# Gathered rows on the memory of the output weights, seven gate-and-up buffers and three transpose banks in a mixture-of-experts stage

## Chip, cores and metric

The kernel runs on one NeuronCore of a Trainium2 chip. The metric is the device time of one execution in microseconds (us). The engines are TensorE (PE; its weight loads are PEld), VectorE (DVE), ScalarE (ACT), GpSimd (POOL) and SyncE (SP), which issues most DMAs.

## What is computed

One step of a hybrid decoder layer for 1024 prompt tokens and 32 sample tokens (1056 in all, width 1024, fp32): an input projection, two parallel attentions, an output projection with a residual, and a two-level mixture of experts. Only the last part bears on the change:

```python
def hier_moe(x, w_rg, b_rg, w_re, b_re, w_g, w_u, w_d):
    ...                                    # a group of 8 experts per token, then its top 2 experts
    dense_gate = jnp.sum(jax.nn.one_hot(ids, N_EXPERTS) * gates[..., None], axis=1)
    hg = jnp.einsum('nd,edf->nef', x, w_g)          # 32 experts, d = 1024, f = 256
    hu = jnp.einsum('nd,edf->nef', x, w_u)
    act = jax.nn.silu(hg) * hu * dense_gate[..., None]
    return jnp.einsum('nef,efd->nd', act, w_d)
...
h = x + mixed @ w_out
return h + hier_moe(rms_norm(h, g_ffn), ...)
```

## The kernel before

Everything runs once, unrolled. A planner of the tile framework orders the instructions of each engine while the program is built: what comes earlier in the program goes first, unless its model of the engines says that it isn't ready and something later is. At run time each engine and each DMA queue goes through its list in order.

**Projection and routing.** The loop over `order` (sample tile first, then eight prompt tiles of 128 rows) runs `project(t)`: the attention's output times `w_out` in three matmuls per chunk (L1328 to L1330, weights `woh`, `wol`), plus the residual, into `h`, which is stored to a DRAM table `hnd` and to the output `yd`. The last tile's stores go through POOL (L1341). L1344 is a small power on POOL for the norm of each tile. `route(t)` (L1346 on) finds two experts per token and their places in lists of 96 slots per expert. `woh` and `wol` fill 64 KB of each partition; when the last projection has been traced, `p3w` closes, and pool `xw2` opens on the upper half of that memory, with two buffers for gate and up weights and two for down weights.

**Weights.** `weights(e, part)` (L1253) loads one expert: part 0 is gate and up (two DMAs of 1 MB into one 16 KB buffer, L1274), part 1 is down (1 MB, L1267). There are six buffers of each, four in `xw` and two in `xw2`, used in turn, so that load n waits for the last use of expert n-6. `HOLD` lets the first load of each part that is issued in the loop wait for the slot table `its`: a one-column copy on POOL into the buffer (L1266, L1272), behind which SP's queue stands.

**Group 0.** The first 32 slots of four experts are known two tiles early. `early_slots` gathers their rows, and after the last tile PE does `turn_rows`, `first_products`, `gated`, `turn_hidden`, `second_products` for them (L1478 and L1486 in the rows below that stand at 1073 to 1078 us). The result `yo0` lies in a buffer of tag `xt` in pool `fp` and is added to the output rows by a scattering DMA on POOL with an adding write (`add_rows`, L1489).

**Groups 1 to 23.** Pool `ep` opens where `fp` and `sm` lay when `p3` closes. Its first tiles are the six `xg` buffers, so `xg` 1 and 2 lie on the two `xt` buffers, one of which holds `yo0`. For each group of 128 slots:

- `fetch` (L1449, POOL) gathers 128 rows of `hnd` into `xg`. Slots without a token gather nothing, so each of the six buffers is zeroed once, on DVE (L1599), before its first gather.
- `turn_rows`: two times four transposes on PE into a bank of PSUM (tag `tr`, two banks; L1458), each followed by a copy with a factor on DVE into a half of `xT` (L1459).
- `turned_hidden` of the group before: two transposes on PE into a `tr` bank (L1478), one copy on DVE to `aTe` (L1479).
- `first_products`: 64 matmuls (L1466) into `acc` (two banks); `gated`: one ACT (L1470) and one DVE instruction (L1472), which read `acc`.
- `down` of the group before: 32 matmuls (L1486) into `S` (two times two banks), ACT writes `yo` (L1620, four buffers), POOL adds it to the output (L1489). Adds go one after the other, since they write the same tensor.

A group uses one or two experts: four groups use three. `units_of` asks for the weights when a group first needs them; the planner puts them on SP's queue.

Of the kernel before, what the change touches and what calls it, by code (L numbers as in the profile page):

```python
# [6 lines left out]
F32 = mybir.dt.float32  # L7
# [8 lines left out]
P = 128  # L16
# [106 lines left out]
def build(tc, a, upto=99, dbg=None):  # L123
# [1120 lines left out]
    xw = p4.enter_context(tc.tile_pool(name="xw", bufs=1, reuse_waits="tile"))  # L1244
    WG, WD = (4, 6), (4, 6)
    xw2 = []
    NEARLY = ((1, 4), (1, 5), (0, 4))
    HOLD = (1, 1)
    XG, YO = 6, 4
    SPREAD = (1, 1, 2, 3, 4, 4, 6, 6)  # L1250
    loaded = [0, 0]

    def weights(e, part, hold=None):  # L1253
# [3 lines left out]
        lim = (WG, WD)[part]  # L1257
        first = n % lim[1] < lim[0]
        pool, bufs = (xw, lim[0]) if first else (xw2[0], lim[1] - lim[0])

# [47 lines left out]
    def project(t):  # L1308
# [34 lines left out]
        V.tensor_scalar(s1[:n, 1:2], s1[:n, 0:1], 1.0 / D, EPS, op0=ALU.mult, op1=ALU.add)  # L1343
        G.tensor_tensor(out=s1[:n, 2:3], in0=s1[:n, 1:2], in1=nhalf[:n, 0:1], op=ALU.pow)  # L1344

# [177 lines left out]
    for i, t in enumerate(order):  # L1523

        pj = project(t)
        last, route_ = route_, None
        step(pj)
        if last:
            step(last)
        step(pj)  # L1530
        if last:
            step(last)
        step(pj)
        route_ = route(t, *hs[t])
        step(route_)
        step(pj)
        if last:
            step(last)
        if i == len(order) + EARLY:
            early_slots()  # L1540
        if i == NT:

            p3w.close()
            xw2.append(p4.enter_context(tc.tile_pool(name="xw2", bufs=1, side="right", reuse_waits="tile")))
            for part, e in NEARLY:
                W_[(part, e)] = weights(8 * (e % 4) + e // 4, part)
        for part, e in ahead.get(i, ()):
            W_[(part, e)] = weights(8 * e, part)

    step(route_)  # L1550
    x0T = turn_rows(xg0s[0], lambda: fp.tile([P, KC, P], F32, name="mx"))
# [28 lines left out]
    V.tensor_scalar(cnti[:, 1:2], cnti[:, 0:1], 7, None, op0=ALU.arith_shift_right)  # L1580
    hid = fp.tile([P, D], F32, name="xt")
    gated(it0[:, 0], gu0, hid[:, :256], hid[:, 256:512])
# [3 lines left out]
    second_products(py0, aT0, u0)  # L1586
    yo0 = fp.tile([P, D], F32, name="xt")
    for q in range(2):
# [3 lines left out]

    psum(2)
    ep = p4.enter_context(tc.tile_pool(name="ep", bufs=2, reuse_waits="tile"))

    def fetch(it, new=False):
        xg = ep.tile([P, D], F32, name="xg", bufs=XG)
        if new:
            V.memset(xg, 0.0)  # L1599
        fetch_to(it, xg)  # L1600
        return it, xg

    def new_xT():
# [12 lines left out]
    def down(it, aT, units):  # L1616
        py = big()
        second_products([py[:, :512], py[:, 512:]], aT, units)
        yo = ep.tile([P, D], F32, name="yo", bufs=YO)
        S.activation(yo, py, AF.Copy, scale=it[:, 1:2].bitcast(F32))  # L1620
        add_rows(it, yo)
# [17 lines left out]

    fetched = {g: fetch(its[:, g], True) for g in (1, 2)}  # L1640
    add_rows(it0[:, 0], yo0)
    behind = None
# [17 lines left out]
    with tc.If(npass > 0):  # L1660
        nrow = 32 * OVF
        ini = ep.tile([P, D], F32, name="xg", bufs=XG)[:, :3 * (nrow // P)].bitcast(I32).rearrange("p (i c) -> p i c", c=3)
        G.iota(ini[:, :, 0], pattern=[[1, nrow // P]], base=0, channel_multiplier=nrow // P)
        V.tensor_scalar(ini[:, :, 0], ini[:, :, 0], 127, None, op0=ALU.bitwise_and)
        inif = ep.tile([P, D], F32, name="xg", bufs=XG)[:, :nrow // P]
        V.tensor_scalar(inif, ini[:, :, 0], float(NTOK), None, op0=ALU.add)
# [58 lines left out]
```

## Time and profile before

| | us |
|---|---|
| median of 3 runs (1405.79 to 1407.11) | 1406.47 |
| profiled execution | 1398.5 |
| its span, first to last instruction | 1396.7 |
| PE busy in the span (90%) | 1258.1 |
| DVE busy (57%) | 801.4 |
| POOL busy (32%) | 447.7 |

The profile is of one execution. Starts are counted from the span's start. A line of a timeline has the start, the duration (of a merged run of equal instructions, to its end), the engine, the line of the kernel, the operation, what it writes and reads, how many, and in brackets how long the engine stood idle before it and what released it. A letter q behind an engine's name is its instruction queue.

### The profile page before, as it was taken

What the parts mean: (1) busy time and instruction counts of PE and PEld (TensorE: products, weight loads), DVE (VectorE), ACT (ScalarE), POOL (GpSimd) and SP (SyncE); (2) the same over time, 40 slices, a digit from 0 to 9 for tenths busy, and PEclk for the clock granted to TensorE, in tenths of its full rate; (3) what the DMA queues carried; (4) which work ended last, traced back from release to release, by engine and by line L of the source; (5) the groups of instructions that cost most, each with busy time, mean ns of one, the idle gap of its engine ahead of it and who ended that gap; (6) DMA issues with size and microseconds to landing.
All of it is one profiled execution on the core that took longest, in us unless ns stands there. A gap on an engine that the chain in (4) does not pass through costs nothing. (4 is left out here: it accounts for less than half of the span.)

```text
span 1396.7 us, 24892 instructions
## 1 busy us (share of the span) xinstructions
PE 1258.1 (90%) x9393; PEld 842.8 (60%) x9393; DVE 801.4 (57%) x2232; ACT 561.7 (40%) x1240; POOL 447.7 (32%) x505
## 2 busy tenths in 40 slices
PE   7999999997789689898889989999998799999994
PEld 5877675875467576675675776768884233333331
DVE  5545996969987677676655556836653311122210
ACT  5533666895432365544445555722221011111110
POOL 1012233254336534335237644322121212222101
PEclk9999999998899799999999999999999899999997
DMA  7223004133325865666558653357636699999962
GB/s 245 68 90 123 25 24 121 48 110 74 99 98 142 233 245 214 232 212 234 178 199 283 222 167 129 92 188 289 248 117 229 235 386 396 396 389 384 391 216 36
DMA packets 114294, 272.60 MB, mean 195 GB/s; under 512 B 52600, under 2 KB 52856, under 8 KB 101880
## 3 DMA queue, kind: packets, MB, share of 16 engines
q1 hardware_dynamic: 81248, 180.84, 35.5%
q0 software_dynamic: 26272, 87.58, 20.0%
q10 hardware_dynamic: 6648, 2.54, 0.7%
q8 instruction: 75, 1.23, 0.3%
q14 instruction: 51, 0.42, 0.1%
HBM read 234.33 MB, written 44.44 MB: 200 GB/s over the span
## 5 line engine op out<-in xcount | busy, mean ns | idle before, releaser
L532 PE MATMUL acc<-wh,xh 128*128 128x512 f32 x432 | 174.6, 404 | 13.8 <-ACT wh L508 13.8
L533 PE MATMUL acc<-wh,xl 128*128 128x512 f32 x432 | 172.0, 398 | 0.0
L1466 PE MATMUL acc<-wg,xT 128*32 128x512 f32 x1472 | 164.3, 598 | 0.0
L941 ACT ACTIVATE mk<-mk,mx 128x256 f32<-128x256 f32 (+7 forms) x128 | 99.0, 774 | 83.2 <-DVE mx L939 78.8
L535 PE MATMUL acc<-wl,xh 128*128 128x512 f32 x320 | 126.5, 395 | 0.0
L1472 DVE SCALAR_TENSOR_TENSOR ac<-acc,its,sg 128x256 f32<-128x256 f32 x23 | 15.8, 688 | 165.1 <-ACT sg L1470 165.1
L532 PEld LDWEIGHTS acc<-wh,xh 128*128 128x128 f32 x432 | 82.5, 191 | 46.3 <-ACT wh L508 22.1
L1466 PEld LDWEIGHTS acc<-wg,xT 128*32 128x32 f32 x1472 | 45.6, 110 | 101.8 <-issue 101.5
L533 PEld LDWEIGHTS acc<-wh,xl 128*128 128x128 f32 x432 | 82.5, 191 | 17.3 <-issue 1.2
L1470 ACT ACTIVATE sg<-acc,its 128x256 f32<-128x256 f32 x23 | 10.9, 473 | 194.7 <-PE acc L1466 194.7
L1486 PE MATMUL S<-wd,aTe 128*32 128x512 f32 x736 | 83.2, 592 | 0.6 <-DVE aTe L1479 0.6
L1105 PE MATMUL tr<-cst,pg 128*128 128x128 f32 x512 | 78.9, 287 | 0.5 <-DVE ql L407 0.4
L937 PE MATMUL tr<-KS,qh 128*128 128x512 f32 (+3 forms) x192 | 74.0, 390 | 1.5 <-DVE aT L865 0.7
L959 POOL TENSOR_SCALAR mk<-mk,rl 128x128 f32<-128x128 f32 (+7 forms) x64 | 49.1, 780 | 69.2 <-DVE rl L951 64.1
L1449 POOL DMA_INDIRECT xg<-s_hn,its x23 | 23.5, 1022 | 140.3 <-PE tr L1458 122.8
L877 PE MATMUL tr<-cst,mk 128*128 128x128 f32 x432 | 64.9, 281 | 3.9 <-POOL mk L959 2.4
L535 PEld LDWEIGHTS acc<-wl,xh 128*128 128x128 f32 x320 | 60.7, 190 | 11.7
L1489 POOL DMA_INDIRECT out_o_y_dram<-yo,its x23 | 36.2, 1576 | 91.7 <-ACT yo L1620 52.1
L1105 PEld LDWEIGHTS tr<-cst,pg 128*128 128x128 f32 x512 | 61.6, 147 | 6.4 <-issue 1.2
L938 PE MATMUL tr<-KS,ql 128*128 128x512 f32 (+3 forms) x192 | 65.1, 353 | 0.0
L1459 DVE TENSOR_TENSOR xT<-tr,gc 128x512 f32<-128x512 f32 x46 | 29.7, 686 | 60.6 <-PE tr L1458 60.6
L877 PEld LDWEIGHTS tr<-cst,mk 128*128 128x128 f32 x432 | 48.5, 142 | 21.8 <-issue 13.5
(447 smaller groups left out, 2913.9 us busy)
## 6 DMA issues: line engine op xcount, KB each, us to landing
wg<-in_w_exp_gate_dram SPq DMA_DIRECT2D x32, 1024.0 KB
wg<-in_w_exp_up_dram SPq DMA_DIRECT2D x32, 1024.0 KB
wd<-in_w_exp_down_dram SPq DMA_DIRECT2D x32, 1024.0 KB
wr<-in_w_in_dram SPq DMA_DIRECT2D x56, 256.0 KB
xt<-in_x_prompt_dram SPq DMA_DIRECT2D x16, 512.0 KB
s_mix<-mo SPq DMA_DIRECT2D x16, 256.0 KB
qn<-s_qa SPq DMA_DIRECT2D x8, 512.0 KB
raw<-in_w_out_dram SPq DMA_DIRECT2D x16, 256.0 KB
```

The lines of the kernel that those rows point to most:

```text
L532: T_.matmul(ps, lhsT=xh[t][:, kc, :], rhs=wh[kc], start=kc == 0 and t < NT - 1, stop=False)
L533: T_.matmul(ps, lhsT=xl[t][:, kc, :], rhs=wh[kc], start=False, stop=t == NT - 1 and kc == KC - 1)
L535: T_.matmul(ps, lhsT=xh[t][:, kc, :], rhs=wl[kc], start=False, stop=kc == KC - 1)
L877: T_.transpose(pt[:, (j - b) * P:(j - b + 1) * P], src[:, j * P:(j + 1) * P], ident)
L937: T_.matmul(sp[:, :c1 - c0], lhsT=T.qh[:, h * P:(h + 1) * P], rhs=KS[:, h, c0:c1], start=True, stop=False)
L938: T_.matmul(sp[:, :c1 - c0], lhsT=T.ql[:, h * P:(h + 1) * P], rhs=KS[:, h, c0:c1], start=False, stop=True)
L941: S.activation(mk[:, :W], mk[:, :W], AF.Exp, bias=mx[:, h:h + 1], scale=-1.0, accum_out=T.ll[:, h:h + 1])
L959: G.tensor_scalar(ex[s][:, :W], ex[s][:, :W], T.rl[:, 2 * u + s:2 * u + s + 1], 1.0, op0=ALU.mult, op1=ALU.mult)
L1105: T_.transpose(pt[:, c * P:(c + 1) * P], raws[bb][:, o_:o_ + P], ident)
L1466: T_.matmul(gu[c:c + m, :].rearrange("p (u f) -> p u f", u=2), lhsT=xT[:, k, c:c + m], rhs=wg[:, :, k, :], start=k == 0, stop=k == KC - 1)
L1486: T_.matmul(py[q][c:c + m], lhsT=aT[:, k, c:c + m], rhs=wd[:, k, q * 512:(q + 1) * 512], start=k == 0, stop=k == 1)
L1489: G.indirect_dma_start(out=yd, out_offset=bass.IndirectOffsetOnAxis(ap=it[:, 0:1], axis=0), in_=yo, in_offset=None, compute_op=ALU.add, bo ...
```

## The change

Gathered rows get a pool of their own, `xg`, on the lower quarter of the memory that `woh` and `wol` held (four buffers of 4 KB; six before, in `ep`). The first two are zeroed on POOL by instructions that the planner must put behind the last L1344 on that engine; buffers 3 and 4 are zeroed on POOL too, where the planner likes. `yo` has two buffers in place of four, and the first of them is allocated before all else in `ep`. `hid` and `yo0` of group 0 use the tag `mh` in place of `xt`. Gate and up weights get a seventh buffer, in `ep`, behind `yo`, that is, over `hT`, both `mh` buffers and one `mx` buffer of `fp`. Loads 5 and 6 of gate and up are asked for between the first two gathers and `add_rows(it0)`, load 5 with the wait for `its`, and the count of held loads is lowered. `psum(3, 1)` gives three banks to `tr` and one to `acc`.

```diff
@@ -1242,11 +1242,11 @@
     p4 = ExitStack()
     cq = p4.enter_context(tc.tile_pool(name="cq", bufs=1))
     xw = p4.enter_context(tc.tile_pool(name="xw", bufs=1, reuse_waits="tile"))
-    WG, WD = (4, 6), (4, 6)
+    WG, WD = (4, 6, 7), (4, 6, 6)
     xw2 = []
     NEARLY = ((1, 4), (1, 5), (0, 4))
     HOLD = (1, 1)
-    XG, YO = 6, 4
+    XG, YO = 4, 2
     SPREAD = (1, 1, 2, 3, 4, 4, 6, 6)
     loaded = [0, 0]
 
@@ -1255,8 +1255,8 @@
         n = loaded[part]
         loaded[part] += 1
         lim = (WG, WD)[part]
-        first = n % lim[1] < lim[0]
-        pool, bufs = (xw, lim[0]) if first else (xw2[0], lim[1] - lim[0])
+        i = n % lim[2]
+        pool, bufs = (xw, lim[0]) if i < lim[0] else (xw2[0], lim[1] - lim[0]) if i < lim[1] else (xw2[2], lim[2] - lim[1])
 
         def src(nm):
             return a[nm][0, e] if isinstance(e, int) else a[nm][0, bass.ds(e, 1)].rearrange("o k n -> (o k) n")
@@ -1341,7 +1341,9 @@
             st.dma_start(dst[r0:r0 + n], h[:n])
         V.tensor_tensor(out=s1[:n, 0:1], in0=s1[:n, 0:1], in1=s1[:n, 1:2], op=ALU.add)
         V.tensor_scalar(s1[:n, 1:2], s1[:n, 0:1], 1.0 / D, EPS, op0=ALU.mult, op1=ALU.add)
-        G.tensor_tensor(out=s1[:n, 2:3], in0=s1[:n, 1:2], in1=nhalf[:n, 0:1], op=ALU.pow)
+        last_pow[0] = G.tensor_tensor(out=s1[:n, 2:3], in0=s1[:n, 1:2], in1=nhalf[:n, 0:1], op=ALU.pow).ins
+
+    last_pow = [None]
 
     def route(t, h, s1):
 
@@ -1542,11 +1544,17 @@
 
             p3w.close()
             xw2.append(p4.enter_context(tc.tile_pool(name="xw2", bufs=1, side="right", reuse_waits="tile")))
+            xw2.append(p4.enter_context(tc.tile_pool(name="xg", bufs=XG, side="right", reuse_waits="tile")))
             for part, e in NEARLY:
                 W_[(part, e)] = weights(8 * (e % 4) + e // 4, part)
         for part, e in ahead.get(i, ()):
             W_[(part, e)] = weights(8 * e, part)
 
+    with tc.issue_after(last_pow[0]):
+        xgs = []
+        for _ in range(2):
+            xgs.append(xw2[1].tile([P, D], F32, name="xg"))
+            G.memset(xgs[-1], 0.0)
     step(route_)
     x0T = turn_rows(xg0s[0], lambda: fp.tile([P, KC, P], F32, name="mx"))
     step(route_)
@@ -1578,27 +1586,34 @@
     cnti = cq.tile([P, 2], I32, name="cnti")
     V.tensor_scalar(cnti[:, 0:1], cnt[:, 32:33], float(P - 1 - CAP), None, op0=ALU.add)
     V.tensor_scalar(cnti[:, 1:2], cnti[:, 0:1], 7, None, op0=ALU.arith_shift_right)
-    hid = fp.tile([P, D], F32, name="xt")
+    hid = fp.tile([P, D], F32, name="mh")
     gated(it0[:, 0], gu0, hid[:, :256], hid[:, 256:512])
     aT0 = hid[:, 512:768].rearrange("p (k n) -> p k n", k=2)
     turn_hidden(hid[:, 256:512], aT0)
     py0 = [acc(), acc()]
     second_products(py0, aT0, u0)
-    yo0 = fp.tile([P, D], F32, name="xt")
+    yo0 = fp.tile([P, D], F32, name="mh")
     for q in range(2):
         S.activation(yo0[:, q * 512:(q + 1) * 512], py0[q], AF.Copy, scale=it0[:, 0, 1:2].bitcast(F32))
     p3.close()
 
 
-    psum(2)
+    psum(3, 1)
     ep = p4.enter_context(tc.tile_pool(name="ep", bufs=2, reuse_waits="tile"))
 
     def fetch(it, new=False):
-        xg = ep.tile([P, D], F32, name="xg", bufs=XG)
-        if new:
-            V.memset(xg, 0.0)
+        if xgs:
+            xg = xgs.pop(0)
+        else:
+            xg = xw2[1].tile([P, D], F32, name="xg")
+            if new:
+                G.memset(xg, 0.0)
         fetch_to(it, xg)
         return it, xg
+
+
+    yos = [ep.tile([P, D], F32, name="yo", bufs=YO)]
+    xw2.append(ep)
 
     def new_xT():
         return ep.tile([P, KC, P], F32, name="xT")
@@ -1616,7 +1631,7 @@
     def down(it, aT, units):
         py = big()
         second_products([py[:, :512], py[:, 512:]], aT, units)
-        yo = ep.tile([P, D], F32, name="yo", bufs=YO)
+        yo = yos.pop() if yos else ep.tile([P, D], F32, name="yo", bufs=YO)
         S.activation(yo, py, AF.Copy, scale=it[:, 1:2].bitcast(F32))
         add_rows(it, yo)
 
@@ -1638,6 +1653,8 @@
         return units
 
     fetched = {g: fetch(its[:, g], True) for g in (1, 2)}
+    W_[(0, 5)], W_[(0, 6)] = (weights(8 * (n % 4) + n // 4, 0, its[:, 1, 0:1] if n == 5 else None) for n in (5, 6))
+    held[0] -= 1
     add_rows(it0[:, 0], yo0)
     behind = None
     for g in range(1, NG + 2):
@@ -1659,10 +1676,10 @@
     npass = nc.values_load(cnti[0:1, 1:2], min_val=0, max_val=8)
     with tc.If(npass > 0):
         nrow = 32 * OVF
-        ini = ep.tile([P, D], F32, name="xg", bufs=XG)[:, :3 * (nrow // P)].bitcast(I32).rearrange("p (i c) -> p i c", c=3)
+        ini = xw2[1].tile([P, D], F32, name="xg")[:, :3 * (nrow // P)].bitcast(I32).rearrange("p (i c) -> p i c", c=3)
         G.iota(ini[:, :, 0], pattern=[[1, nrow // P]], base=0, channel_multiplier=nrow // P)
         V.tensor_scalar(ini[:, :, 0], ini[:, :, 0], 127, None, op0=ALU.bitwise_and)
-        inif = ep.tile([P, D], F32, name="xg", bufs=XG)[:, :nrow // P]
+        inif = xw2[1].tile([P, D], F32, name="xg")[:, :nrow // P]
         V.tensor_scalar(inif, ini[:, :, 0], float(NTOK), None, op0=ALU.add)
         V.tensor_copy(ini[:, :, 0], inif)
         V.memset(ini[:, :, 1:], 0)
```

## Rows read from the trace of the kernel before

**Rows 1.** Windows, all engines: stretch; busy us (instructions) per engine; clock; DMA share; GB/s

```profile
1075.00:1110.00 35.00, 20.68 (x166) 7.26 (x162) 9.00 (x12) 1.85 (x3) 9.71 (x9) 0.80 0.63 206
...
1180.00:1215.00 35.00, 33.98 (x306) 12.04 (x302) 6.70 (x12) 4.76 (x6) 6.69 (x6) 1.00 1.02 391
...
1343.00:1346.00 3.00, 3.00 (x36) 0.91 (x32) 0.57 (x1) 0.47 (x1) 0.00 (x0) 1.00 0.55 168
```

**Rows 2.** Timeline of PE, from group 0 to group 3

```profile
1074.03 3.64 PE L1486 MATMUL acc<-wd,xt 128*32 128x512 f32 x32 [0.52 <-DVE xt L1479]
1091.22 1.97 PE L1458 MATMUL tr<-cst,xg 128*128 128x128 f32 x8 [13.55 <-DMA xg<-s_hn,its]
1093.12 8.69 PE L1466 MATMUL acc<-wg,xT 128*32 128x512 f32 x64
1101.74 1.16 PE L1458 MATMUL tr<-cst,xg 128*128 128x128 f32 x8
...
1114.47 1.16 PE L1458 MATMUL tr<-cst,xg 128*128 128x128 f32 x8
1115.97 0.44 PE L1478 MATMUL tr<-cst,ac 128*128 128x128 f32 x2 [0.34 <-DVE xT L1459]
1116.33 7.08 PE L1466 MATMUL acc<-wg,xT 128*32 128x512 f32 x64
1123.22 3.62 PE L1486 MATMUL S<-wd,aTe 128*32 128x512 f32 x32
```

**Rows 3.** Timeline of DVE between group 0 and group 1

```profile
1071.67 0.20 DVE L1445 COPY its<-low 128x48 f32<-128x48 f32 x1
...
1085.49 0.91 DVE L1599 MEMSET xg<- 128x1024 f32 x1 [11.52 <-DMA out_o_y_dram<-xt,it]
...
1092.37 0.69 DVE L1459 TENSOR_TENSOR xT<-tr,gc 128x512 f32<-128x512 f32 x1 [0.60 <-PE tr L1458]
1093.23 0.69 DVE L1459 TENSOR_TENSOR xT<-tr,gc 128x512 f32<-128x512 f32 x1 [0.16 <-PE tr L1458]
```

**Rows 4.** Timeline of POOL in the same stretch

```profile
1060.35 0.56 POOL L1344 TENSOR_TENSOR s<-s,nhalf 128x1 f32<-128x1 f32 x1 [0.48 <-DVE b L1430]
1071.88 0.19 POOL L1272 CAST wg<-its 128x1 f32<-128x1 int32 x1 [10.97 <-DVE its L1445]
1078.72 1.71 POOL L1489 DMA_INDIRECT out_o_y_dram<-xt,it  x1 [6.65 <-ACT xt L1589]
1087.20 1.06 POOL L1449 DMA_INDIRECT xg<-s_hn,its  x1 [6.78 <-DVE xg L1599]
```

**Rows 5.** Windows of PE alone: stretch, length, busy us (instructions), clock, DMA share, GB/s

```profile
1094.00:1096.00 2.00, 2.00 (x16) 0.50 0.89 271
```

**Rows 6.** Waits of PE, 1102 to 1376 us: in total us, times, longest

```profile
PE tr L1478 <- DVE xT L1459: 7.5, 21, 0.8
```

**Rows 7.** Timeline of SP's queue: weight loads

```profile
1101.85 0.33 SPq L1274 DMA_DIRECT2D wg<-in_w_exp_gate_dram  x1
...
1312.96 0.33 SPq L1274 DMA_DIRECT2D wg<-in_w_exp_up_dram  x1
...
1336.02 0.33 SPq L1267 DMA_DIRECT2D wd<-in_w_exp_down_dram  x1
```

**Rows 8.** Timeline of POOL: two adds in a row

```profile
1277.51 1.59 POOL L1489 DMA_INDIRECT out_o_y_dram<-yo,its  x1 [0.65 <-issue]
...
1290.81 1.59 POOL L1489 DMA_INDIRECT out_o_y_dram<-yo,its  x1 [1.64 <-DMA out_o_y_dram<-yo,its]
```

**Rows 9.** Timelines of DVE and POOL: one DVE instruction beside POOL and without it

```profile
1042.58 2.36 POOL L176 TENSOR_TENSOR mx<-mx,mh 128x1024 fp32r<-128x1024 f32 x1 [2.63 <-ACT mh L1316]
1043.72 1.24 DVE L1371 TENSOR_SCALAR c<-lg,g 128x4 f32<-128x4 f32 x1
1062.46 0.22 DVE L1371 TENSOR_SCALAR c<-lg,g 128x4 f32<-128x4 f32 x1
```

**Rows 10.** Groups of POOL's instructions by line and form: a zeroing of the same size

```profile
L1084 POOL MEMSET QB<- 128x1024 f32 x2 | 1.9, 962 | 1.7 <-PE tr L1121 1.7
```

## The prediction

> **What bounds the kernel now.** I read the busy slices of the page first: DMA is full over the last sixth of the span and TensorE (PE) is at nine tenths nearly everywhere, with one weak place just ahead of that last sixth. The windows show it: from 1075 to 1110 us PE works 20.7 of 35 us at a mean clock of 0.80, while a window of the experts' loop has 34.0 of 35 at full clock [rows 1]. So there are two losses, a hole ahead of the loop and about 1 us in 35 within it. DMA share is 1.02 in the loop [rows 1], so the weights must be watched as well.
>
> The hole: group 0 ends on PE at 1077.67 (1074.03 + 3.64), and group 1's transposes begin at 1091.22, after 13.55 us of waiting for gathered rows [rows 2]. The gather was asked for at 1087.20 and waited for its zeroing [rows 4]; the zeroing started at 1085.49 and waited 11.52 us for the adding DMA that reads `yo0` [rows 3], since the first `xg` buffers lie on the two `xt` buffers. That DMA was asked for at 1078.72 [rows 4]. The slot table that a gather needs was there at 1071.87 [rows 3], and POOL did something that needs it at 1071.88 [rows 4]. So the gather is held for 15.3 us by memory alone.
>
> The clock: after that idle time PE runs at a granted clock of 0.50, that is 1.2 of 2.4 GHz, for instance from 1094 to 1096 [rows 5].
>
> The loop: in a steady group the two transposes of the hidden rows wait 0.34 us for DVE's first copy into `xT` [rows 2], because with two banks they need the one which that copy empties. The wait is 7.5 us in 21 groups [rows 6], 0.357 each. Nothing else of PE's waiting in the loop is worth naming.
>
> **The change part by part.**
>
> *Gathered rows off `ep`, `yo0` onto `mh`.* Only L1330 and its kind read the old weights, and they end with the last projection, before 1060.35, where the last L1344 stands. Gathers 1 and 2 need the table (1071.87) and POOL, which is idle for 10.97 us before 1071.88 [rows 4]. A gather took 4.02 us from issue to the start of the waiting transposes (1087.20 to 1091.22) [rows 2, 4]; issued at 1071.9 its rows are there at 1075.9, and PE is free at 1077.67. So PE goes on at 1077.7 at the earliest: 13.5 us gained, and what is late next is PE itself, by 1.7 us. If the gather takes longer than that, the price is one for one.
>
> *The clock after the hole.* From the first transpose of group 1 to that of group 2 it took 10.52 us (1091.22 to 1101.74) [rows 2]. At full clock: 1.50 from the first transpose to the moment when the first copy is there (1114.47 to 1115.97), and 6.89 for the 64 matmuls (1116.33 to 1123.22) [rows 2], together 8.39. That is 2.13 us, if the clock stays up. PE's pauses while it finishes group 0 are there before too, and after 1077.7 no idle time is left. Together with the hole: group 2 starts at 1086.1 in place of 1101.74, 15.6 us earlier.
>
> *Three `tr` banks, one `acc` bank.* The hidden rows' transposes (0.36 us from their start to that of the first products, 1115.97 to 1116.33 [rows 2]) then run in the time of the wait. The first products need the first half of `xT` only: in group 1 they began at 1093.12, before the second copy began at 1093.23 [rows 2, 3]. They would start just after the first copy, where the hidden transposes start now: 0.30 to 0.36 a group, 0.33 taken, times 22 groups is 7.3 us. One `acc` bank costs nothing: the hidden transposes of group g-1, which stand ahead of group g's first products on PE, need what `gated` made out of that bank, so it has been read by then.
>
> *Zeroing on POOL.* Two instructions of 0.96 us [rows 10] behind the last L1344, from 1060.9 to 1062.8, in idle POOL time; two more where the planner likes. DVE loses six of 0.91 in the hole [rows 3], where nobody but the gather waited. But DVE works at the last tile's routing then, which ends in the slot table. The trace shows what POOL does to it: L1371 took 1.24 us beside a POOL instruction that ended at 1044.94, and 0.22 us without one [rows 9]. So the cost lies between nothing and 1.9 us; the routing has small pauses, I take 0.5. That L176 reads two operands and a zeroing none speaks for the low end. The Trainium skill, page "SBUF — State Buffer", section "SBUF: two separate sides", has a rule that speaks against this part: VectorE and GpSimd hold their shared port pair exclusively, and the later one blocks for the whole instruction. The trace agrees, with the 1.24 us; by the rule the four zeroings could cost up to 3.8 us, and the sum would be 19 in place of 22.4.
>
> *Loads 5 and 6.* Load 5 waits for the copy on POOL, now behind two gathers of about 1.06 us [rows 4], some 2.6 us later than at present; it is first used in group 3, over 20 us away. Load 6 goes to memory under `yo0` and waits for its add, to about 1085.5 [rows 3]; SP has nothing behind it that could go sooner, since load 7 needs group 1's first products (1086.1). Before, the stream of loads began again at 1101.85 [rows 7]. So it moves 16.4 us ahead, and PE 15.6.
>
> *Does the stream keep up?* DMA is full, at 391 GB/s, and delivers a group's share in about the 12.3 us that a group takes (1.02 share throughout [rows 1]); PE would want it in 11.97. Before: the second half of expert 29 was asked for at 1312.96, and group 21 needs it at 1116.33 + 18 x 12.3 = 1337.7. A load lands 8 to 13 us after issue (the last was issued at 1336.02, and DMA has fallen to half by 1343 to 1346 [rows 1, 7]; the upper figure is an estimate from five loads in flight at the spacing of the queue). So 12 us are in hand. After: 12 + 0.8 - 18 x 0.33 = 7 us. It keeps up, with less to spare.
>
> *Four `xg` and two `yo` buffers.* A gather can be issued when the transposes four groups earlier are done, some 48 us before use, against the 4 us that the first one took with DMA half idle. `yo` g+2 waits for add g; an add that was waited for took 13.3 us from start to start (1277.51 to 1290.81) [rows 8], and two groups are 24. Both cost nothing as long as adds don't pile up.
>
> **Sum:** 13.5 + 2.1 + 7.3 - 0.5 = 22.4 us. The profiled execution took 1398.5 (span 1396.7 and 1.8 around it) and would take 1376.1. The median of the runs shown is 8.0 higher than the profiled one, 1406.47; the change comes off that too: 1384.
>
> **The rivals.**
>
> *The weights come late.* PE wants weights faster than a full DMA delivers them. For it: the share of 1.02, and the sum above leaves only 7 us. Against: the first weights start 16 us sooner. If a group's transfers took 12.8 us in place of 12.3, 18 x 0.5 = 9 us would be needed of 7, and 2 us lost; if all of the loop's gain went, 1391. Time: 1386 to 1391, say 1389. The same time comes out if the third bank only moves the wait to the first products.
>
> *The first rows come late.* Should POOL do load 5's copy ahead of the gathers, 2 MB of weights (5.4 us at 391 GB/s) share DMA with the first rows; PE then waits up to 4 us, and the clock may fall as in rows 5, for 2.1 more. Time: 1386 to 1390.
>
> *The hole stays.* If a tile of group 1 still lies over `yo0`, only the loop's 7.3 us come: 1399. Against: `xg` is on other memory, and `yo0` lies in `fp` behind `xt` and `hT`, where by the order of allocation only load 6 comes to lie.
>
> *Slower: the adds.* Adds go one after the other, and with two `yo` buffers ACT, then `S`, then PE would wait if adds took longer than a group. At 13.3 us each [rows 8] the loop would go at 13.3: 22 x 1.0 lost against 12.3, and the 15.1 of the rest gained, 1413. It decides from 12.3 + 15.1/22 = 13.0 us for a mean add. Against: the add at 1277.51 didn't wait for its forerunner [rows 8], so at present the mean is at most a group's 12.3, with four buffers that do nothing for it.
>
> **How the numbers follow.** Forecast 0.66 (its own range 1381 to 1387: the unknowns above, and what the planner may shift); weights late 0.14; first rows late 0.12; hole stays 0.04, half of it with other losses that bring it to no change; adds 0.04. The time is 1384. The range 1380 to 1393 holds the forecast and both middle rivals. About 0.2%, some 3 us, is what a measurement can tell from no change: faster 0.94, within it 0.02, slower 0.04.
>
> **What the profile would show.** Right: gathers on POOL at about 1072 to 1074, group 1's transposes right behind group 0's last matmul with under 1 us of idle time, clock 1.00 there, a group every 11.97 us, no wait of L1478 for `xT` but one of the order of 0.05 us at L1466. Wrong: idle PE ahead of L1466 or L1486 released by a weight DMA (weights late); idle time at the first L1458 released by `xg`'s DMA, clock 0.50 (first rows late); L1620 or L1486 waiting for an add (adds); L1371 and its neighbours at 1 us and more (zeroing).

## The result

| | before | changed |
|---|---|---|
| median of the timed runs (4 each, one chip), us | 1406.79 | 1395.22 |
| profiled execution, us (span) | 1398.5 (1396.7) | 1391.4 (1389.6) |

The ratio is 0.9916, with a 95% interval of 0.9893 to 0.9939: 11.6 us saved, about half of the 22.4 of my sum, and 1395 lies above my range. On a second chip the ratio was 0.9922 (0.9909 to 0.9935), 11.6 us again.

Starts can't be compared: at the last projection the profiled execution of the changed kernel is already 5 us later than that of the kernel before, with the same instructions up to there, and the second one of the changed kernel, on the second chip, gets to group 0's first products at 1038.43 where the first one does at 1066.66 us. So I compare distances between landmarks on PE. The helper's lines are two higher than before the change: L1460 and L1461 are `turn_rows`, L1468 the first products, L1480 and L1488 the hidden rows' transposes and the second products, L1491 the add.

Windows of the changed kernel, with the columns of [rows 1]:

```profile
1075.00:1110.00 35.00, 31.67 (x321) 12.56 (x323) 8.65 (x23) 3.91 (x6) 10.17 (x11) 1.00 0.72 254
1180.00:1215.00 35.00, 34.42 (x312) 20.14 (x310) 6.69 (x12) 3.96 (x6) 7.86 (x6) 1.00 1.02 394
...
1320.00:1355.00 35.00, 33.05 (x290) 16.51 (x282) 6.13 (x11) 4.76 (x6) 3.14 (x3) 1.00 0.64 225
```

Against [rows 1], the stretch ahead of the loop has 31.7 us of PE work in place of 20.7, and the clock there is 1.00 in place of 0.80. The middle of the loop rose only from 33.98 to 34.42. The new thing is the last row: late in the loop PE works 1.4 us less than in the middle.

PE of the changed kernel, from group 0 to group 2:

```profile
1073.37 0.41 PE L1409 MATMUL low<-oh,cst 128*128 128x32 f32 x2 [2.23 <-DVE oh L1401]
...
1081.34 3.64 PE L1488 MATMUL acc<-wd,mh 128*32 128x512 f32 x32 [0.52 <-DVE mh L1481]
1084.91 1.16 PE L1460 MATMUL tr<-cst,xg 128*128 128x128 f32 x8
1086.43 0.71 PE L1460 MATMUL tr<-cst,xg 128*128 128x128 f32 x4 [0.36 <-ACT mh L1597]
1087.07 7.07 PE L1468 MATMUL acc<-wg,xT 128*32 128x512 f32 x64
1094.07 0.71 PE L1460 MATMUL tr<-cst,xg 128*128 128x128 f32 x4
...
1095.82 7.07 PE L1468 MATMUL acc<-wg,xT 128*32 128x512 f32 x64
```

The hole of [rows 2] is gone: group 1's transposes stand right behind group 0's last matmul, and four of group 2's run early in the third bank. From the end of group 0 to group 1's first products it is 2.1 us in place of 15.4 (1077.67 to 1093.12), and from there to group 2's 8.75 in place of 10.91, since the clock stays up. New is the wait of 2.23 us ahead, in the last tile's routing. DVE and POOL there:

```profile
1065.92 3.67 DVE L1433 TENSOR_SCALAR b<-b,cst 128x2 f32<-128x2 f32 x1
1066.05 3.54 DVE L1461 TENSOR_TENSOR mx<-tr,gc 128x512 f32<-128x512 f32 x1
```
```profile
1065.95 1.83 POOL L1557 MEMSET xg<- 128x1024 f32 x2
1067.73 1.84 POOL L1610 MEMSET xg<- 128x1024 f32 x2
```

The planner put all four zeroings in a row, and one DVE instruction on 128x2 elements lasts as long as the four.

The loop: the end of group 1, a steady group, and then the two worst late ones:

```profile
1102.71 3.62 PE L1488 MATMUL S<-wd,aTe 128*32 128x512 f32 x32
1106.26 1.16 PE L1460 MATMUL tr<-cst,xg 128*128 128x128 f32 x8
...
1163.19 3.76 PE L1488 MATMUL S<-wd,aTe 128*32 128x512 f32 x32
1166.88 1.16 PE L1460 MATMUL tr<-cst,xg 128*128 128x128 f32 x8
1167.87 0.38 PE L1480 MATMUL tr<-cst,ac 128*128 128x128 f32 x2
1168.46 7.19 PE L1468 MATMUL acc<-wg,xT 128*32 128x512 f32 x64 [0.21 <-DVE xT L1461]
...
1302.65 1.05 PE L1468 MATMUL acc<-wg,xT 128*32 128x512 f32 x4 [0.21 <-DVE xT L1461]
1304.32 6.63 PE L1468 MATMUL acc<-wg,xT 128*32 128x512 f32 x58 [0.61 <-DMA wg<-in_w_exp_up_dram]
...
1328.43 1.06 PE L1468 MATMUL acc<-wg,xT 128*32 128x512 f32 x6 [0.16 <-issue]
1330.86 6.62 PE L1468 MATMUL acc<-wg,xT 128*32 128x512 f32 x57 [1.37 <-SPq L1677]
```

The wait of the hidden rows' transposes [rows 6] is gone, and a group takes 12.11 us in place of 12.30. But three late groups (18, 19 and 21) take 13.07, 13.68 and 14.43 us, 4.9 us too much in all, as their first products stop after a few matmuls. SP's queue shows what they wait for:

```profile
1300.80 0.33 SPq L1274 DMA_DIRECT2D wg<-in_w_exp_gate_dram  x1
1304.25 0.33 SPq L1267 DMA_DIRECT2D wd<-in_w_exp_down_dram  x1
1306.67 0.33 SPq L1274 DMA_DIRECT2D wg<-in_w_exp_up_dram  x1
```

These are expert 29's gate half, expert 28's down load and expert 29's up half (counted from the end of the queue). The trace's completion records have the last part of the up half at 1330.81; PE goes on at 1330.86. So a load lands 24 us after its issue here, and each issue follows the landing of the load eight before it (1306.67 that of the load of 1280.71, recorded at 1306.66). So eight loads of 1 MB share the DMA, and at 394 GB/s these are 21 us, by estimate most of the 24. The releaser in that row, SP's queue, is only the event nearest to the landing.

From group 2's to group 23's first products, 21 groups, it was 258.4 us before and 259.2 in the changed kernel (260.0 in its second profile). The whole gain of the loop was given back at its end:

| landmark | before | changed | second profile |
|---|---|---|---|
| wait at L1409 | 0 | 2.2 | 2.2 |
| end of group 0 to group 1's first products | 15.4 | 2.1 | 1.5 |
| group 1's to group 2's first products | 10.9 | 8.8 | 8.8 |
| group 2's to group 23's | 258.4 | 259.2 | 260.0 |

The differences add up to 12.4 and 12.2 us saved; the timed runs say 11.6.

### The profile page after: what moved, and what is told of

Read it like the earlier page. It is cut to its first block, busy times and chain, and to the rows that moved or that the text cites. A ratio compares the mean times of both kernels' runs of the same rounds, so it can differ in the third digit from the quotient of the medians.

```text
span 1389.6 us, 24897 instructions
## 1 busy us (share of the span) xinstructions
PE 1260.6 (91%) x9393; PEld 897.3 (65%) x9393; DVE 796.3 (57%) x2226; ACT 561.7 (40%) x1240; POOL 452.9 (33%) x509
## 5 line engine op out<-in xcount | busy, mean ns | idle before, releaser
L1468 PE MATMUL acc<-wg,xT 128*32 128x512 f32 x1472 | 167.8, 593 | 6.1 <-DVE xT L1461 2.9
L1468 PEld LDWEIGHTS acc<-wg,xT 128*32 128x32 f32 x1472 | 80.9, 110 | 77.3 <-issue 62.7
L1488 PE MATMUL S<-wd,aTe 128*32 128x512 f32 x736 | 88.1, 592 | 0.6 <-DVE aTe L1481 0.6
L1472 ACT ACTIVATE sg<-acc,its 128x256 f32<-128x256 f32 x23 | 10.9, 473 | 178.8 <-PE acc L1468 178.8
L1461 DVE TENSOR_TENSOR xT<-tr,gc 128x512 f32<-128x512 f32 x46 | 29.7, 686 | 65.0 <-PE tr L1460 64.9
L1488 PEld LDWEIGHTS S<-wd,aTe 128*32 128x32 f32 x736 | 43.2, 110 | 36.5 <-issue 34.4
L340 POOL TENSOR_TENSOR m<-raw,gtab 128x512 f32<-128x512 f32 x32 | 47.5, 1486 | 48.9 <-ACT raw L377 35.9
```

Source lines behind the costliest of these rows:

```text
L340: last_rot[0] = (V if n == NS else G).tensor_tensor(out=m2[:n, :w].rearrange('p (h u d) -> p h u d', u=2, d=32), in0=sv[:, :, ::-1, :], in ...
L1468: T_.matmul(gu[c:c + m, :].rearrange("p (u f) -> p u f", u=2), lhsT=xT[:, k, c:c + m], rhs=wg[:, :, k, :], start=k == 0, stop=k == KC - 1)
L1488: T_.matmul(py[q][c:c + m], lhsT=aT[:, k, c:c + m], rhs=wd[:, k, q * 512:(q + 1) * 512], start=k == 0, stop=k == 1)
```

## Experiments

Theory after this result: the hole and the clock came as forecast, the zeroing cost 2 us, and the third bank's gain of some 4 us was lost again to weights that come late. Rival: the third bank or the zeroing does something else, and the late stalls have another cause. The kernel before took 1377 to 1407 us on the chips used, so each run is judged by its ratio to the runs of the kernel before beside it. "21 groups" is the distance from group 2's to group 23's first products in the run's profile; without a stall that is 254.3 us at 12.11 us a group and 258.4 at 12.30. Differences from the changed kernel are taken from its second ratio, 0.9922.

| kernel | ratio | 95% interval | 21 groups, us |
|---|---|---|---|
| changed, first and second time | 0.9916, 0.9922 | 0.9893 to 0.9939, 0.9909 to 0.9935 | 259.2, 260.0 |
| two banks | 0.9899 | 0.9879 to 0.9920 | 258.3 |
| half down loads, three banks | 0.9880 | 0.9861 to 0.9900 | 254.3 |
| half down loads, two banks | 0.9928 | 0.9907 to 0.9949 | 258.3 |
| before, with three banks | 1.0012 | 1.0001 to 1.0023 | 259.6 |
| six gate and up buffers | 0.9946 | 0.9929 to 0.9963 | 262.3 |
| zeroing elsewhere | 0.9909 | 0.9894 to 0.9923 | 256.5 |
| early load 6, first layout | 0.9951 | 0.9937 to 0.9965 | 259.3 |
| the same, zeroing elsewhere | 0.9948 | 0.9936 to 0.9961 | 257.7 |
| early load 6, second layout | 0.9911 | 0.9894 to 0.9929 | 259.2 |
| down loads later | 0.9895 | 0.9874 to 0.9916 | 257.1 |
| all three | 0.9860 | 0.9838 to 0.9882 | 254.3 |

**The changed kernel again.**

> The changed kernel itself, once more, beside the same runs of the kernel before as the next three. Theory (the change is worth what its timed runs showed, and the 5 us by which its profiled execution stood behind the other at 1062 us are drift between executions): again 10 to 13 us under the kernel before, and a second profile that reaches the wait of L1409 at another moment, but with the same 2.2 us in it, group 1's transposes right behind group 0's last matmul, a group every 12.1 us, and the same stalls of 1 to 2.5 us in the first products of groups 17 to 21. Rival (the 5 us are a cost of the change in the attention): the profile reaches the last projection late again by 5 us or more.

11.6 us under the kernel before, with the same wait and stalls. Whether the 5 us at the last projection are drift this profile can't say: it gets to group 0's first products 28 us earlier than the first one, but on a chip where the kernel before is faster by 30 us too. Other profiles speak for drift. On one chip the kernel before with three banks gets there at 1041.24 us and three kernels with the change at 1039.18 to 1040.08; and on another, two kernels whose instructions are the same up to there do at 1038.43 and 1043.97.

**What is the third bank worth?** Three kernels. Two banks in the changed kernel:

```diff
-    psum(3, 1)
+    psum(2)
```

> The changed kernel with two banks for transposes and two for acc, as before the change; all else is kept (the planner shifts a few weight loads in the queue). Theory (TensorE waits for weights at the end, and the third bank gains 0.16 us a group): a group takes 12.3 us again, the 0.36 us wait of the hidden rows' transposes is back, TensorE is 3.4 us later at group 17, and the stalls of 4.7 us shrink by as much: 0 to 1.5 us above the changed kernel. Rival (the third bank is worth the 7.3 us that I had put down for it): 7 us above it.

Half of each down load from the seventh on, with three banks; the other half of these weights is not loaded:

```diff
-            Y.dma_start(w, src("w_exp_down").rearrange("(p c) n -> p c n", p=P))
-            return w
+            f = D if n < 6 or not isinstance(e, int) else 512
+            Y.dma_start(w[:, :, :f], src("w_exp_down").rearrange("(p c) n -> p c n", p=P)[:, :, :f])
+            return w if f == D else w[:, :, :f]
...
-                    T_.matmul(py[q][c:c + m], lhsT=aT[:, k, c:c + m], rhs=wd[:, k, q * 512:(q + 1) * 512], start=k == 0, stop=k == 1)
+                    T_.matmul(py[q][c:c + m], lhsT=aT[:, k, c:c + m], rhs=wd[:, k, q * 512 % wd.shape[2]:q * 512 % wd.shape[2] + 512], start=k == 0, stop=k == 1)
```

> The changed kernel with half of each down-projection load from the seventh on: the second half of those weights isn't loaded and the second half of the output columns is computed with the first half's weights, so a sixth of the weight bytes is left out and the work of the engines is the same. Theory (the stalls in groups 17 to 20 are bytes that come late): no wait of L1468 for weights is left, time 4 to 5 us under the changed kernel; a group still takes 12.1 us, if it is TensorE's own weight loads that took back half of the third bank's gain, or 11.97 if a full DMA did. Rival (the stalls come from something else): stalls and time as in the changed kernel.

And the same with `psum(2)`:

> The kernel with half of each down load from the seventh on (second half of those weights not loaded, the second half of the output columns computed with the first half's weights), and two banks for transposes and two for acc in place of three and one. Together with the run that has three banks it prices the third bank where weights are no limit. Theory (0.18 us a group): a group takes 12.30 us and the time is 4 us above that of the same kernel with three banks. Rival (0.33 us a group, as in my sum): 7 us above it. If the third bank were worth nothing even so: the same time.

Waits of PE in the loop (in total us, times, longest): first of the half-load kernel with three banks, then with two. Lines are one higher here than in the changed kernel.

```profile
PE acc L1469 <- DVE xT L1462: 2.9, 14, 0.2
PE acc L1469 <- issue: 1.0, 6, 0.2
PE S L1489 <- DVE aTe L1482: 0.6, 1, 0.6
```
```profile
PE tr L1481 <- DVE xT L1462: 7.5, 21, 0.8
```

With fewer bytes no wait for a weight is left, the time falls by 0.4%, some 5.8 us, and the 21 groups take 12.11 us on the mean: the stalls are bytes that come late. There the third bank is worth 4.0 us in the profile (258.3 to 254.3); the timed runs say 6.7, with an error of some 4. With all bytes it is worth nothing: two banks are not slower than three (0.9899 against 0.9922). The rival with 7.3 us falls by the profiles, and by the ratios of the pair with all bytes; the timed runs of the half-load pair alone would not exclude it.

The head of a group, from the first transpose to the first products, takes 1.58 us (1166.88 to 1168.46) in place of 1.86 [rows 2]: the wait of 0.34 us ahead of the hidden rows' transposes is gone, and one of 0.21 us behind them is new. The tail, from the second products to the next transposes, takes 3.69 (1163.19 to 1166.88), where group 1 of the same kernel took 3.55 (1102.71 to 1106.26). PE's weight loads are busy for 20.1 us of 35 there, where it was 12.0 [rows 1]. The last loads of a group's second products and the first ones of the next transposes, in the kernel before and then in the changed one:

```profile
1138.10 0.13 PEld L1486 LDWEIGHTS S<-wd,aTe 128*32 128x32 f32 x4 [0.30 <-issue]
1139.07 0.97 PEld L1458 LDWEIGHTS tr<-cst,xg 128*128 128x128 f32 x8 [0.84 <-issue]
```
```profile
1165.77 0.27 PEld L1488 LDWEIGHTS S<-wd,aTe 128*32 128x32 f32 x4 [0.16 <-issue]
1166.88 0.97 PEld L1460 LDWEIGHTS tr<-cst,xg 128*128 128x128 f32 x8 [0.84 <-issue]
```

Four loads that took 0.13 us are spread over 0.27, and in both kernels the next load starts 0.84 us behind the last of them: that is the 0.14 us by which the tail is longer. With half the down loads a group takes 12.11 us too, also from 1290 to 1320 us of that run, where DMA share is 0.30; so a full DMA is not the cause. Why the loads spread was not tried.

**The bank alone, in the kernel before.**

```diff
-    psum(2)
+    psum(3, 1)
```

> The kernel before with one edit, three banks for transposes and one for acc. Theory (before, the last weights came only some 1.2 us ahead of their use): the loop's turn falls from 12.30 to 12.14 us, 3.4 us in 21 groups, of which TensorE waits 2 back for weights at the end: 1 to 2 us under the kernel before. Rival (12 us in hand before, as I had it, and 0.33 us a group): 7 us under it.

No gain: 1.7 us slower, where I had expected 1 to 2 faster. PE in the group with the larger of two stalls:

```profile
1277.93 1.06 PE L1466 MATMUL acc<-wg,xT 128*32 128x512 f32 x6 [0.17 <-issue]
1282.37 6.60 PE L1466 MATMUL acc<-wg,xT 128*32 128x512 f32 x57 [3.38 <-DMA wg<-in_w_exp_up_dram]
```

The two groups last 1.0 and 4.3 us longer than 12.1; that is 5.3 us lost for 4 gained; why more is lost than gained is not shown. So before the change the weights had almost nothing in hand.

**One buffer less.**

```diff
-    WG, WD = (4, 6, 7), (4, 6, 6)
+    WG, WD = (4, 6, 6), (4, 6, 6)
...
-    W_[(0, 5)], W_[(0, 6)] = (weights(8 * (n % 4) + n // 4, 0, its[:, 1, 0:1] if n == 5 else None) for n in (5, 6))
+    W_[(0, 5)] = weights(8 * (5 % 4) + 5 // 4, 0, its[:, 1, 0:1])
```

> The changed kernel with six gate and up buffers and no early load 6; load 5 stays where it is. Theory (the stream of weights has about no time in hand at the end, so a buffer of 2 MB less costs up to the 5.4 us that it takes to move): 2 to 5 us above the changed kernel, by larger stalls in the first products of the last groups. Rival (load 6 starts no earlier than group 1's products would have freed an old buffer, and a full DMA moves the same bytes in the same time whatever the number of buffers): within 1 us.

3.3 us above the changed kernel by the ratios (the intervals overlap a little), and one group takes 7.9 us too long, as the theory has it. But this profile shows something else as well: with the same PE, DVE and POOL instructions as in the changed kernel up to there, group 2's rows came late (a line of PE):

```profile
1062.90 0.68 PE L1460 MATMUL tr<-cst,xg 128*128 128x128 f32 x4 [3.41 <-DMA xg<-s_hn,its]
```

The gather was asked for at 1054.73, so it took 8.2 us, in place of the 4.0 that I had from the kernel before [rows 2, 4]; behind the wait the clock was low, and from group 1's to group 2's products it took 10.5 us in place of 8.8. In this profile the late rows cost 5.4 us against the second profile of the changed kernel, and the 21 groups 2.3 us more than that one's. So the price of the buffer alone is not shown.

**Zeroing off GpSimd.** Two buffers on ScalarE behind the last squares, two on VectorE behind group 0's copy of the turned hidden rows; else the same order. The lines that set `last_sq` are left out here.

```diff
-            G.memset(xgs[-1], 0.0)
+            S.activation(xgs[-1].rearrange("p (k n) -> p k n", n=P), ident.unsqueeze(1).to_broadcast([P, KC, P]), AF.Copy, scale=0.0)
...
-                G.memset(xg, 0.0)
+                with tc.issue_after(last_sq[0]): V.memset(xg, 0.0)
```

> The changed kernel with its zeroing off GpSimd: buffers 1 and 2 by two instructions on ScalarE, buffers 3 and 4 by two on VectorE behind group 0's copy of the turned hidden rows. All else is in the same order. Theory (GpSimd's zeroing holds VectorE up for 3.6 us in the last tile's routing, and 2.2 of them reach TensorE): L1409 no longer waits 2.2 us, the routing instructions beside L1434 take 0.2 us again, group 1's first products come 2 us earlier; of that only what the weights don't take back at the end is seen, so the time is 0 to 2.2 us under the changed kernel. Rival (the wait at L1409 has another cause, or the routing was not on the path): the wait stays, time the same.

PE of this kernel:

```profile
1040.51 0.41 PE L1409 MATMUL low<-oh,cst 128*128 128x32 f32 x2
...
1048.48 5.34 PE L1488 MATMUL acc<-wd,mh 128*32 128x512 f32 x32 [0.52 <-DVE mh L1481]
1053.75 1.16 PE L1460 MATMUL tr<-cst,xg 128*128 128x128 f32 x8
1056.01 0.68 PE L1460 MATMUL tr<-cst,xg 128*128 128x128 f32 x4 [1.10 <-DMA xg<-s_hn,its]
```

The wait at L1409 is gone, so GpSimd's zeroing was its cause. But group 0's second products take 5.34 us in place of 3.64, as the clock falls to 0.50 in them, and rows come 1.10 late: group 1 starts 20.5 us after group 0's first products, as in the changed kernel (20.4 and 19.8). So the time won at L1409 is not seen here. The 1.8 us by which the ratio is better lie within the two intervals. What is better in this profile is the loop, with one stall of 2.2 us in place of three: load 7 was issued 7.1 us after group 1's first products began, in place of 9.0 and 11.2.

**Load 6 earlier.** First try: the seventh buffer as the first tile of `ep`, `yo0` in an `mx` buffer.

```diff
-    yo0 = fp.tile([P, D], F32, name="mh")
+    yo0 = fp.tile([P, D], F32, name="mx")
...
-    yos = [ep.tile([P, D], F32, name="yo", bufs=YO)]
+    yos = []
```

> The changed kernel with the seventh gate and up buffer on memory that is free early: it becomes the first tile of ep and lies on xt, xt, hT and the first mh buffer; yo0 takes an mx buffer in place of an mh buffer. The order of instructions is the same on every engine. Theory (the weights come late at the end since their stream stands still until yo0's add is done, 8 us behind TensorE's start of group 1): load 6 is issued at about 1083 in place of 1095 us, the stream is ahead by up to one load, 2 MB or about 5 us, and the stalls of 4.7 us in groups 17 to 20 shrink to under 1: 3 to 5 us under the changed kernel. Rival (the stalls have another cause, such as a late DMA engine or a slow queue that is there whatever the start): within 1 us of the changed kernel, with stalls of the same size in the same groups.

4 us slower than the changed kernel: a miss of my edit. ACT and PE:

```profile
1079.14 0.47 ACT L1472 ACTIVATE sg<-acc,its 128x256 f32<-128x256 f32 x1 [14.46 <-DMA out_o_y_dram<-mx,it]
```
```profile
1080.37 0.69 PE L1480 MATMUL tr<-cst,ac 128*128 128x128 f32 x2 [7.27 <-DVE ac L1474]
```

The tiles of group 1's `gated` (`sg`, `ac`) now lay over `yo0` and waited for its add, and PE waited for them: the trap that the change had removed, at a new place. Two of the three late stalls were gone, though. The kernel with the zeroing moved as well has the same fault, so its result says nothing beyond that:

> Both edits of the last two kernels together. Theory: TensorE comes to group 1 2 us earlier and the weights are ahead by 5 us, so both gains are seen: 5 to 7 us under the changed kernel, and the fastest of all. Rival (the end is set by the DMA's throughput alone, from load 7 on): not below the kernel with the early load 6, as the weights take back what the zeroing gives.

The second layout has no such overlap:

```diff
-    yos = [ep.tile([P, D], F32, name="yo", bufs=YO)]
     xw2.append(ep)
...
-    held[0] -= 1
+    held[0] -= 1; yos = [ep.tile([P, D], F32, name="yo", bufs=YO)]
```

> The changed kernel with two lines exchanged: the seventh gate and up buffer is the first tile of ep and the first yo buffer stands behind it. So the buffer lies on xt, xt, hT and the first mh buffer (which holds hid), and yo0 lies under the first yo buffer, not under anything that group 1 needs early, which was the fault of the earlier trial. The order of instructions is the same on every engine. Theory (the stream stands still for yo0's add): load 6 is issued when group 0's second products end, some 10 us earlier, load 7 right behind group 1's first products, 4 to 5 us earlier, group 1 and 2 run as in the changed kernel, and the stalls of groups 17 to 21 shrink from 4.7 to 5.8 us to under 2: 3 to 5 us under the changed kernel. Rival (moving load 6 into the time of the first gathers and of yo0's add makes these later): the gated step of group 1 or the rows of group 2 wait for several us, and the time is that of the changed kernel or above.

Load 6 went out at about 1080 and load 7 at 1088.58, 7.1 us after group 1's first products began, as hoped. The stalls of groups 18 and 19 are gone. Yet the time is that of the changed kernel, because group 21 now stops for longer:

```profile
1320.24 1.06 PE L1468 MATMUL acc<-wg,xT 128*32 128x512 f32 x6 [0.16 <-issue]
1323.80 8.06 PE L1468 MATMUL acc<-wg,xT 128*32 128x512 f32 x57 [2.49 <-SPq L1676]
```

PE comes to this group 2.6 us earlier, counted from group 1's first products (238.8 against 241.4 us), and expert 29's up half lands only 1.5 us earlier (242.3 against 243.7). The clock falls again behind the stall (8.06 in place of 6.6 us). My theory of a gain of 3 to 5 us fell; what was right is only that an earlier start moves the stalls.

**The order of the loads.** The down load of an expert goes behind the next expert's gate and up loads.

```diff
-    W_ = {}
+    W_, ups = {}, []
...
-            for part in range(2):
-                if (part, n) not in W_:
+            for part, m in ((0, n), (0, min(n + 1, 31)), (1, n)):
+                if (part, m) not in W_:
...
-            Y.dma_start(w, src("w_exp_down").rearrange("(p c) n -> p c n", p=P))
+            with tc.issue_after(ups[-1]) if 5 < n < 32 else ExitStack(): Y.dma_start(w, src("w_exp_down").rearrange("(p c) n -> p c n", p=P))
...
-            Y.dma_start(w[:, u], src(nm).rearrange("(p c) f -> p c f", p=P))
+            ups.append(Y.dma_start(w[:, u], src(nm).rearrange("(p c) f -> p c f", p=P)).ins)
```

> The changed kernel with another order in the queue of weight loads: the down load of expert n stands behind the gate and up loads of expert n+1 (it is needed a whole group later than they are). All engines' own instructions are in the same order. Theory (the stalls are the wrong load coming first: expert 29's up half stands behind expert 28's down load, which is needed some 19 us later, and costs 2.5 us of DMA time): the stall of group 21 goes, the others shrink, 2 to 5 us under the changed kernel. Rival (the stream as a whole is late, whatever its order): the stalls stay at 4 us or more in sum, or move to the second products, and the time is within 1 us.

By the ratios 3.7 us under the changed kernel (the intervals overlap a little), by the profile 2 to 3 in the 21 groups. Group 21 loses 1.5 us in place of 2.3, the others 1.3 in place of 2.5.

**All three edits.**

> The changed kernel with the three edits that each may gain: early load 6, down loads behind the next expert's gate and up loads, zeroing on ScalarE and VectorE. Theory: no stall for weights is left and a group takes 12.1 us to the end, 5 to 8 us under the changed kernel, the fastest of all. Rival (DMA's throughput sets the end: the last load lands some 264 to 267 us after group 1's first products begin, whatever comes before): not more than 3 us under the changed kernel, with the stall at another place.

The fastest: 1379.8 us against 1400.1 of the kernel before, 20.3 us, and 8.5 under the changed kernel by the ratios. PE of groups 21 and 22:

```profile
1318.80 7.15 PE L1468 MATMUL acc<-wg,xT 128*32 128x512 f32 x64 [0.16 <-issue]
1325.67 3.72 PE L1488 MATMUL S<-wd,aTe 128*32 128x512 f32 x32
...
1330.90 7.22 PE L1468 MATMUL acc<-wg,xT 128*32 128x512 f32 x64 [0.21 <-DVE xT L1461]
```

No stall is left, and the loop takes the 254.3 us that it takes with a sixth of the weight bytes left out. The up half of expert 29 landed at 1318.70, one tenth of a microsecond ahead of these products, which read it from the seventh matmul on. So three edits worth 1.5, 1.8 and 3.7 us alone give 8.5 together (the sum is 7.0, and each of these numbers has an error of 2 to 3 us), and with that the loop stands about where PE and DMA end alike.

## Why the prediction was wrong

- *The hole* (13.5 us): right. 13.4 and 14.0 us less from the end of group 0 to group 1's first products, no wait for rows in the changed kernel's profiles. "4.02 us from issue" was the price with DMA less than half busy (share 0.41 from 1087 to 1091 us); with load 5 beside it, at a share of 1.01, it was 8.2 in one run. So my 1.7 us of cover were thin, and that no wait is seen is in part luck.
- *The clock* (2.1 us): right together with the hole. From the end of group 0 to group 2's first products it is 15.5 and 16.1 us less, and 15.6 in the kernel with two banks; I had 15.6. That the table's 10.9 and 8.8 differ by 2.1 too is partly chance: with two banks the second number is 9.3, and the third bank lets four of group 2's transposes run ahead.
- *Zeroing* (0.5 us): mis-sized. The two bounds were zero and 1.9; the wait is 2.23. I reasoned that two of the four would fall where the planner likes, and that an instruction with no operands would hold DVE less. The rows above show DVE held for all 3.6 us. The rule of the Trainium skill, page "SBUF — State Buffer", section "SBUF: two separate sides", by which a GpSimd instruction can keep VectorE from the port pair that they share until it ends, was the better guide here. The trace agrees with it, with DVE's 3.67 us beside POOL's 1.83 and 1.84.
- *Three banks* (7.3 us): the wait went as forecast, but two things were wrong. The first is the size: 0.19 us a group, not 0.33. On the mean of groups 5 to 17 the head gained 0.29 (the wait left at the first products is 0.21 us, where I had 0.05), the first products 0.03, and 0.14 was lost at the tail, which no step of mine looked at. That is 4 us, where weights are no limit. The second is the next step.
- *Does the stream keep up?* This is the step that failed. "A load lands 8 to 13 us after issue" came from five loads in flight at the spacing of the queue; it was an estimate, and no row bore it. The loads land 24 us after issue, with eight in flight and not five. So for the load of 1312.96 [rows 7], needed at 1337.7, not 12 us were in hand but about one (two, as group 21 reads it from its seventh matmul on): its last part is recorded at 1336.46. That DMA share was 1.02 and that a group's bytes took as long as a group [rows 1] had said so already. A PE that gains 0.19 us a group, 3.4 us in 18, must then stall, and did: the three-bank kernels with all bytes lose from 2.0 to 8.0 us to it, until the order and the start of the loads were changed together.
- *Load 6*: right in the difference that counts. I had the stream move 16.4 us ahead and PE 15.6. Load 6 was issued at 1095.1, when the add of `yo0` was done, 8.0 us after group 1's first products began; before, the stream began 8.7 us after them [rows 2, 7]. So it gained 0.7 us on PE, and I had 0.8. But I took that for safety, and it is nothing against what the loop's gain asks of it.
- *The rivals*: "the weights come late" is what happened. I gave it 0.14 and priced it at 1386 to 1391; with the loop's gain gone and 1.7 us more for the zeroing, the sum is 13.4 us and the time 1393, and the end of the loop takes 1 to 2 more. The chance was too low: what stood against it was a start 16 us sooner, which PE's own earlier start takes back, and the 7 us in hand, which rested on the estimate. *First rows late* showed in two profiles of variants, *the adds* in none.

## What to carry over

When DMA is full through a loop, ask for each late load when it was issued and when it was needed, and take the time from issue to landing from a pair of rows, not from the spacing of the queue: with eight loads in flight it was 24 us here, at a spacing of some 3. A gain on the engine that consumes such a stream is worth only what the stream has in hand; here the order in the queue (what is needed first goes first) and an earlier start had to come with it, and with them the engine's own gain was seen in full. And memory that a scattering DMA still reads is a wait for whatever is laid over it next; look at what moves there when a tile moves away.

## What the hardware showed that I had not expected

- A weight load has 16 completion records; late in the changed kernel's loop the first and the last of them lie 17 to 24 us apart. The last three loads still take 23 to 25 us to land, in a stretch where the mean DMA share is 0.64.
- With the same PE instructions, the clock fell to 0.50 in the thin stretch of the last tile's routing in some executions and not in others: the 19 matmuls there take 2.35 us in the changed kernel and 3.87 in the half-load run, whose instructions are the same up to there. Such a dip costs 1.5 to 1.7 us, and some runs have it later, in group 0's second products (5.34 us for 3.64, in one run 6.36).
- Behind the stalls of 2.49 and 4.25 us (early load 6, six buffers) the clock is at 0.50 for a while, and the rest of the first products takes 8.06 and 9.32 us in place of 6.6; behind the one of 3.38 us it is not.
- The same kernel before had medians from 1377 to 1407 us on the chips that were used.
